# Queueing the taps of a depthwise convolution on VectorE behind given instructions of the MLP

## The chip, the cores and the metric

One core of a Trainium2 chip runs the whole network in one launch. The metric is the device time of that core in microseconds (us), the median over the runs shown; lower is better.

## What is computed

The input x is 1024 tokens by 1024 channels, float32, and goes through two layers and a last rmsnorm. Layer 0 is a hybrid mixer (a recurrence beside sliding-window attention) and an MLP; layer 1 is a convolution module and an MLP. The change touches what lies between the mixer's output and the second MLP. Cut to that:

```python
def conformer_conv(h, ...):
    u = h @ pw1_w + pw1_b
    u = u[..., :D_MODEL] * jax.nn.sigmoid(u[..., D_MODEL:])
    u = depthwise_conv(u, dw_w) + dw_b        # causal, 31 taps per channel
    u32 = layernorm(u, ln_g, ln_b)            # over the channels
    u = jax.nn.silu(u32)
    return u @ pw2_w + pw2_b

def sqrelu_mlp(h, w1, w2):                    # 1024 -> 4096 -> 1024
    return jnp.square(jax.nn.relu(h @ w1)) @ w2

x = x + mix;  x = x + sqrelu_mlp(rmsnorm(x), w1, w2)    # in each layer
```

## The kernel before, in words

Tokens are handled in two halves of 512, with channels on the 128 partitions: a half is eight tiles of 128x512 (`x0` for the first half, `x1` for the second). Every float32 product is made of three matmuls (`mm3`, lines 296 to 301): a number is split into a high part and the rest, and high by high, high by low and low by high are added up in PSUM. The high part is a cast on ScalarE (line 286 for weights), the low part a subtraction (`lo`, line 271), which goes to VectorE or to GpSimd by an argument; with `dve=False` it goes to GpSimd.

Weights come through SyncE's DMA queue into rings of four tiles for the raw values, the high and the low parts (`weights`, lines 273 to 291). One weight block of 8x128 channels uses two tiles of each ring, so at most two blocks are there at a time, and they come in the order of the program. Matmul results go to a ring of six PSUM banks (`self.mm`, line 1436).

The work around the change, in the order of the program (`run`, from line 1446):

- `conv_in(0)` (lines 1199 to 1217): the first projection of the convolution for the first half, eight channel tiles of 48 matmuls; each ends in one VectorE instruction that writes `u[c]` (line 1217).
- `mlp(0)` on `x1` (lines 1137 to 1196): eight blocks of 512 hidden channels. `first` makes a hidden piece (24 matmuls, then relu, square and the high part on ScalarE, the low part at line 1165 on GpSimd). `second` takes a block back to the channels in four groups of 24 matmuls; each group ends in two VectorE additions into `x` (line 1183), which also give two PSUM banks free. With `ahead` 2 the order is: four pieces; then for each block two pieces of the next, the four groups of this one, the other two pieces of the next.
- `conv(us, acc0)` (lines 1219 to 1227): 31 taps for each of eight channel tiles, 248 VectorE instructions, each `acc = u shifted * weight + acc` (line 1226; the first tap is line 1223).
- `conv_norm` (lines 1233 to 1252): layernorm and silu of the eight `acc` tiles, a chain over VectorE, TensorE (lines 1239 and 426) and ScalarE that ends in eight high and low parts (lines 1250 and 1251).
- `norm(x1)`, `conv_out(0)` (lines 1254 to 1263: eight columns of 24 matmuls, the last product of the convolution), copies of the last 30 columns of each `u[c]` to its front on GpSimd (line 1457).
- the same for the other half: `conv_in(1)`, `mlp(1)` on `x0` for seven of its blocks, `conv` of the second half, `conv_norm`, `conv_out(1)`, then the eighth block and the rest.

Up to the end of the mixer the order on TensorE is written out by hand. From there a planner orders every engine's queue when the kernel is built: it goes through its own estimate of the instructions' times, and gives an engine that is free the ready instruction that stands first in the program. The norms are marked as urgent. `conv` stands behind the whole MLP in the program, but its taps are ready as soon as `u[c]` is there, so the planner puts them on VectorE wherever it believes VectorE free. On the chip each engine then goes through its queue strictly in order.

Of the kernel before, what the change touches and what calls it, by code (L numbers as in the profile page):

```python
# [9 lines left out]
F32 = mybir.dt.float32  # L10
F32R = mybir.dt.float32r
AF = mybir.ActivationFunctionType
ALU = mybir.AluOpType
# [4 lines left out]
P = 128  # L18
D = 1024
S = 1024  # L20
H = 512
# [3 lines left out]
NTAP = 31  # L25
# [8 lines left out]
class Ring:  # L34
    """slots taken in turn, from one or several pools"""
# [10 lines left out]
class Net:  # L46
# [25 lines left out]
    # ---------------------------------------------------------------- order on the tensor engine  # L72
    def go(self, gen):
        """a stream on its own"""
        while True:
            try:
                next(gen)
            except StopIteration as e:
                return e.value

    def weave(self, base, *gens):
        """several streams in one order: the first of gens that is due goes on, base between them, so that the array
        stays busy; a stream yields the time (us) that its next products have to wait for the other engines, or the
        name of what has to be there"""
        due = [[0.0, g] for g in gens]
        rest = [[0.0, base]]
        share = 0.0

        def first(ds):
            return next((d for d in ds if (d[0] in self.done if isinstance(d[0], str) else d[0] <= self.clk)), None)  # L90

        while due or rest:
            f, b = first(due), first(rest)
            d = f if f and (share < LAG["SHARE"] or not b) else b
            if d is None:
                self.clk = min(d[0] for d in due + rest if not isinstance(d[0], str))
                continue
            t = self.clk
            try:
                w = next(d[1])  # L100
                d[0] = w if isinstance(w, str) else self.clk + w + (LAG["SLACK"] if w else 0.0)
            except StopIteration:
                (due if d is f else rest).remove(d)
            t = self.clk - t
            share = share + t if d is f else max(0.0, share - LAG["RATIO"] * t)

    # ---------------------------------------------------------------- constants
# [62 lines left out]
    def warm(self):  # L170
        """products that nobody reads, while the array would only wait: so its clock stays up for the first columns"""
        ps = self.mmps()
        for _ in range(4):
            self.nc.tensor.matmul(ps[:, 0:256], lhsT=self.ones, rhs=self.rst[:, 0:256], start=True, stop=True)
# [89 lines left out]
    # ---------------------------------------------------------------- helpers  # L264
    def lo(self, out, x, hi, dve=None):
        """out = x - hi, for the second part of an operand"""
        if dve is None:
            self.nlo += 1
            dve = self.nlo % 3 != 0
        eng = self.nc.vector if dve else self.nc.gpsimd  # L270
        eng.tensor_tensor(out=out, in0=x, in1=hi.bitcast(F32), op=ALU.subtract)  # L271

    def weights(self, aps, a, b, dve=None):
        """blocks of weights in two parts, k by k; loaded and split one half of them after the other"""
        nc = self.nc
        h = a // 2
        if dve is None:
            self.nlo += 1
            dve = self.nlo % 3 != 0
        ws = [([], []) for _ in aps]  # L280
        for i in range(2):
            for ap, (his, los) in zip(aps, ws):
                raw = self.wraw.tile([P, h, b], F32, "wraw")
                nc.sync.dma_start(out=raw, in_=ap[:, i * h:(i + 1) * h, :])
                hi = self.whi.tile([P, h, b], F32R, "whi")
                nc.scalar.copy(out=hi, in_=raw)  # L286
                lo = self.wlo.tile([P, h, b], F32R, "wlo")
                self.lo(lo, raw, hi, dve)
                his += [hi[:, k, :] for k in range(h)]
                los += [lo[:, k, :] for k in range(h)]  # L290
        return ws
# [30 lines left out]
    def norm_first(self, hf, rows, dst):  # L322
        """first rmsnorm by rows, then turned to feature-major; dst(u, g): where the two parts go"""
# [42 lines left out]
    def first_stored(self):  # L366
        """the second half's first norm, kept in DRAM until its place is free"""
# [20 lines left out]
    def colsum(self, xs, sq, k="n"):  # L388
        """sum over channels of x (or of its square), in two parts"""
# [29 lines left out]
    def rstd(self, accs, eps, pool, k="n"):  # L419
        """1 / sqrt(mean + eps) for every token, on every partition"""  # L420
# [56 lines left out]
    # ---------------------------------------------------------------- input projection  # L477
# [10 lines left out]
    def w_in_pair(self, js, hs):  # L488
        """two columns side by side, channel block by channel block: what is there first is used first"""
# [31 lines left out]
    # ---------------------------------------------------------------- rwkv  # L521
    def scan(self, hf, p, r, k, v, la, gl, sset, ptag, ahead):
# [86 lines left out]
        # unit lower triangular inverse: 16-blocks by substitution, then two merges  # L609
# [97 lines left out]
        # per chunk: state' = M state + C, output = R state + Y  # L707
# [114 lines left out]
    # ---------------------------------------------------------------- attention  # L822
    def attention(self, hf, i, z, qs, mi):
        """query heads 2i and 2i+1"""
# [54 lines left out]
    # ---------------------------------------------------------------- mixer of one half  # L879
# [14 lines left out]
    def shift(self, hf, j, ps, keep=False, hp=False):  # L894
        """one 128-channel column of the input projection of the rwkv part, shifted"""
# [18 lines left out]
    def twice(self, j, rows, cols, width):  # L914
        """64 channels of a column, on both halves of the partitions; cols: (from, of which half's column) pieces"""
# [6 lines left out]
    def att_in(self, hf):  # L922
        """keys with one block of the half before in front: the high part of each kv head on both halves of the
        partitions, the low parts of the first on the upper one and of the second on the lower one; values by rows"""
# [23 lines left out]
    def queries(self, hf, i, z):  # L948
        """two heads' queries, each with its high part on the half of the partitions where the low part of its keys is
        and its low part on the other one"""  # L950
# [10 lines left out]
    def att(self, hf, z):  # L961
        """attention of one half: query heads 4z to 4z+3"""
# [26 lines left out]
    def cols0(self, hs):  # L989
        """the first half's input projection"""  # L990
# [23 lines left out]
    def last1(self, h1):  # L1014
        """the last two columns, under the norm"""
# [20 lines left out]
    def scans(self, z, todo):  # L1036
        """scans one after the other in one set of tiles"""
# [39 lines left out]
    def w_out(self, hf, mi, xs, w_):  # L1077
        """output projection; the second half's input is there, the first half's comes along;
        the first half's first two columns begin with what is done, while the last scan and the attention go on"""
# [56 lines left out]
    # ---------------------------------------------------------------- mlp  # L1136
    def mlp(self, layer, halves, blocks, ahead, dve=None, close=None):
        """halves: list of (x tiles, (hi, lo)); blocks of 512 hidden channels;
        ahead: how many 128-channel pieces of a block go before the second product of the block in front;
        close: takes the second product of the last block"""  # L1140
# [5 lines left out]
        def first(fb, fts):  # L1146
            hid = hids.setdefault(fb, [([], []) for _ in halves])
            for ft in fts:
                f = fb * 4 + ft
                whi, wlo = self.weight(w1[:, :, f * P:(f + 1) * P], NK, P, dve)  # L1150
                for hh, (xs, (his, los)) in zip(hid, halves):
# [13 lines left out]
                    self.lo(lo, t, hi, dve)  # L1165
                    hh[0].append(hi)
                    hh[1].append(lo)

        def second(fb):
            hid = hids.pop(fb)  # L1170
            for oc in range(4):
                whi, wlo = self.weight(w2[:, fb * 4:fb * 4 + 4, oc * 256:(oc + 1) * 256], 4, 256, dve)
                for hh, (xs, _) in zip(hid, halves):
# [7 lines left out]
                    for o in range(2):  # L1181
                        x = xs[oc * 2 + o]
                        nc.vector.tensor_tensor(out=x, in0=pss[o], in1=x, op=ALU.add)  # L1183
# [14 lines left out]
    # ---------------------------------------------------------------- convolution  # L1198
    def conv_in(self, hf, hs, us):
# [3 lines left out]
        for c in range(NK):  # L1203
# [13 lines left out]
            nc.vector.scalar_tensor_tensor(out=u[:, NTAP - 1:], in0=ps, scalar=self.pv("b1", c), in1=t, op0=ALU.add, op1=ALU.mult)  # L1217

    def conv(self, us, accs):
        nc = self.nc  # L1220
        for c in range(NK):
            u, acc = us[c], accs[c]
            nc.vector.tensor_scalar(out=acc, in0=u[:, 0:H], scalar1=self.pv("dw0", c), scalar2=self.pv("db", c),
                                    op0=ALU.mult, op1=ALU.add)
            for j in range(1, NTAP):
                nc.vector.scalar_tensor_tensor(out=acc, in0=u[:, j:j + H], scalar=self.pv(f"dw{j}", c), in1=acc,  # L1226
                                               op0=ALU.mult, op1=ALU.add)

# [36 lines left out]
    def row_rstd(self, ss, n):  # L1265
        """1 / sqrt(mean + eps) from n sums of squares of every row"""
# [10 lines left out]
    def final(self, hf, xs):  # L1277
        """last rmsnorm, by rows again"""
# [19 lines left out]
    def final_rows(self, hf, xs, w2, his, los):  # L1298
        """what is there so far by rows, and the second product of the last block by rows; then the last rmsnorm, one
        block of tokens after the other"""  # L1300
# [50 lines left out]
    # ---------------------------------------------------------------- the whole  # L1351
    def run(self):
# [96 lines left out]
        self.conv_in(0, self.norm(x0, "nm1", 0), us)  # L1449
        self.go(self.mlp(0, [(x1, self.norm(x1, "nf0", 1))], range(8), 2, False))  # L1450
        acc0 = [self.mip.tile([P, H], F32, name="acc", tag="mi") for _ in range(8)]
        self.conv(us, acc0)
# [5 lines left out]
        self.conv_in(1, n1, us)  # L1458
        n0 = self.norm(x0, "nf1", 0)
        self.go(self.mlp(1, [(x0, n0)], range(7), 2, False))  # L1460
        acc1 = [self.mip.tile([P, H], F32, name="acc", tag="mi") for _ in range(8)]
        self.conv(us, acc1)
# [41 lines left out]
```

## Time and profile before

| | |
|---|---|
| runs | 2525.11, 2516.49 and 2522.08 us, median 2522.08 |
| profiled execution, from its first to its last instruction | 2519.2 us (the page gives no other time of that execution) |
| TensorE matmul busy | 2355.4 us, 93% |
| VectorE busy | 1568.6 us, 62% |
| ScalarE busy | 1055.3 us, 42% |
| GpSimd busy | 843.9 us, 33% |
| the 480 taps of line 1226 | 466.7 us of VectorE, 1030 ns each |

Busy time says how long an engine had an instruction in it, not that it worked at its full pace: matmuls overlap in their pipeline, so the pace of TensorE is read from the number of matmuls in a stretch, and an instruction that waits inside an engine for a port counts as busy. The mean granted TensorE clock is 0.968 of full speed.

### The profile page before, as it was taken

Reading aid. Unit: us, or ns where it says so; the run is one execution under the profiler, and the core shown is the slowest. Engines: PE = TensorE matmul, PEld = TensorE weight load, DVE = VectorE, ACT = ScalarE, POOL = GpSimd, SP = SyncE. Lnnn points to the kernel's source line nnn. Section 1 sums busy time; section 2 is a strip of 40 time slices with the busy share of each in tenths; the row PEclk is TensorE's granted clock in tenths of the full one; section 3 lists DMA queues with packets and bytes.
Section 4 is the critical chain, followed back from the end, with each engine's and each line's share of the span. In section 5 each row is a group of like instructions: output and inputs, shape, how many; then the busy total and the mean of one; then the engine's idle time right before and its main releaser. Section 6 shows DMA issues by size and latency. Waiting matters only on the chain.

```text
span 2519.2 us, 38162 instructions
## 1 busy us (share of the span) xinstructions
PE 2355.4 (93%) x14525; PEld 1875.1 (74%) x14525; DVE 1568.6 (62%) x2613; ACT 1055.3 (42%) x1888; POOL 843.9 (33%) x676
## 2 busy tenths in 40 slices
PE   7999899899999999999678999997779999999998
PEld 6776677767777778777566888876657888888887
DVE  6766745647573646499998403899998025533333
ACT  6546645445352424344223543523225434433333
POOL 2223333111111112126547664226456643212221
PEclk9999999989999999999898999999889999999999
DMA  6435324313122223323112333332222332433332
GB/s 210 115 108 147 93 67 147 101 58 90 56 70 85 74 81 101 101 84 101 59 59 76 101 98 99 93 88 84 67 67 80 101 100 88 127 100 96 97 99 85
DMA packets 371851, 236.19 MB, mean 94 GB/s; under 512 B 39522, under 2 KB 355156, under 8 KB 371668
## 3 DMA queue, kind: packets, MB, share of 16 engines
q1 hardware_dynamic: 367604, 225.89, 30.2%
q0 software_dynamic: 2176, 4.19, 0.6%
q10 hardware_dynamic: 1888, 3.67, 0.4%
q8 instruction: 114, 1.87, 0.3%
q14 instruction: 69, 0.57, 0.1%
HBM read 215.35 MB, written 18.35 MB: 93 GB/s over the span
## 4 chain that ended last, share of the span: by engine, by line
PE 64%; DVE 28%; ACT 3%; DMA 3%; issue 2%; SPq 0%; POOL 0%; ACTq 0%; DVEq 0%; POOLq 0%
PE mm L299 19%; PE mm L300 18%; PE mm L301 18%; DVE acc L1226 17%; DVE x L1183 1%; DVE wlo L271 1%; DVE nt L472 1%; PE sc L603 1%; DMA raw<-p 1%; PE sc L685 1%; DVE E L662 1%; DVE C L660 1%; DVE h L271 1%; PE sc L768 1%; PE at L842 1%
## 5 line engine op out<-in xcount | busy, mean ns | idle before, releaser
L271 POOL TENSOR_TENSOR wlo<-wraw,whi 128x512 fp32r<-128x512 f32 x448 | 630.6, 1411 | 1293.6 <-ACT whi L286 1223.3
L286 ACT CAST whi<-wraw 128x512 fp32r<-128x512 f32 x720 | 445.1, 620 | 1065.8 <-PE mm L300 911.0
L299 PE MATMUL mm<-h,whi 128*128 128x512 f32 x1792 | 730.3, 408 | 10.7 <-DVE x L1183 7.1
L301 PE MATMUL mm<-h,wlo 128*128 128x512 f32 x1792 | 707.2, 395 | 7.5 <-DVE wlo L271 7.5
L300 PE MATMUL mm<-h,whi 128*128 128x512 f32 x1792 | 706.4, 394 | 0.5 <-DVE h L271 0.3
L299 PE MATMUL mm<-hidh,whi 128*128 128x512 f32 x992 | 396.0, 401 | 77.0 <-DVE x L1183 75.4
L1226 DVE SCALAR_TENSOR_TENSOR acc<-u,par,acc 128x512 f32<-128x512 f32 x480 | 466.7, 1030 | 0.1
L299 PEld LDWEIGHTS mm<-h,whi 128*128 128x128 f32 x1792 | 340.5, 190 | 93.6 <-issue 18.1
L301 PEld LDWEIGHTS mm<-h,wlo 128*128 128x128 f32 x1792 | 340.4, 190 | 85.3 <-DVE wlo L271 11.6
L301 PE MATMUL mm<-hidh,wlo 128*128 128x512 f32 x992 | 389.8, 395 | 11.2 <-POOL wlo L271 11.2
L300 PEld LDWEIGHTS mm<-h,whi 128*128 128x128 f32 x1792 | 341.3, 190 | 67.8 <-issue 2.0
L300 PE MATMUL mm<-hidl,whi 128*128 128x512 f32 x992 | 390.0, 394 | 0.3 <-DVE hidl L271 0.2
L1183 DVE TENSOR_TENSOR x<-mm,x 128x512 f32<-128x512 f32 x248 | 167.6, 685 | 291.9 <-PE mm L301 291.7
L271 DVE TENSOR_TENSOR wlo<-wraw,whi 128x512 fp32r<-128x512 f32 x272 | 194.6, 717 | 202.7 <-ACT whi L286 194.4
L299 PEld LDWEIGHTS mm<-hidh,whi 128*128 128x128 f32 x992 | 189.3, 191 | 123.1 <-issue 80.7
L301 PEld LDWEIGHTS mm<-hidh,wlo 128*128 128x128 f32 x992 | 189.1, 191 | 52.2 <-POOL wlo L271 11.6
L300 PEld LDWEIGHTS mm<-hidl,whi 128*128 128x128 f32 x992 | 189.6, 191 | 39.8 <-issue 1.1
L271 POOL TENSOR_TENSOR hidl<-rel,hidh 128x512 fp32r<-128x512 f32 x77 | 113.1, 1468 | 44.3 <-ACT hidh L1162 25.1
L1158 ACT ACTIVATE rel<-rel 128x512 f32<-128x512 f32 x128 | 80.6, 632 | 3.5
L1157 ACT ACTIVATE rel<-mm 128x512 f32<-128x512 f32 x128 | 75.5, 592 | 5.9 <-DVE u L1217 4.8
L1164 DVE CAST hidh<-rel 128x512 fp32r<-128x512 f32 x68 | 31.4, 464 | 52.5 <-ACT rel L1158 52.4
L473 ACT CAST h<-nt 128x512 fp32r<-128x512 f32 x48 | 29.7, 621 | 56.9 <-DVE nt L472 56.5
(357 smaller groups left out, 2257.3 us busy)
## 6 DMA issues: line engine op xcount, KB each, us to landing
wraw<-in_mlp_w_dram SPq DMA_DIRECT2D x512, 256.0 KB
wraw<-in_cv_pw_w_dram SPq DMA_DIRECT2D x96, 256.0 KB
wraw<-in_hy_w_in_dram SPq DMA_DIRECT2D x80, 256.0 KB
wraw<-in_hy_w_out_dram SPq DMA_DIRECT2D x32, 256.0 KB
p<-stg SPq DMA_DIRECT2D x30, 256.0 KB
raw<-p SPq DMA_DIRECT2D x40, 128.0 KB
krv<-p SPq DMA_DIRECT2D x18, 256.0 KB
xrow<-in_x_dram SPq DMA_DIRECT2D x8, 512.0 KB
```

The lines of the kernel that those rows point to most:

```text
L271: eng.tensor_tensor(out=out, in0=x, in1=hi.bitcast(F32), op=ALU.subtract)
L286: nc.scalar.copy(out=hi, in_=raw)
L299: mm(ps, lhsT=whi, rhs=xhi, start=start, stop=False)
L300: mm(ps, lhsT=whi, rhs=xlo, start=False, stop=False)
L301: mm(ps, lhsT=wlo, rhs=xhi, start=False, stop=stop)
L472: nc.vector.scalar_tensor_tensor(out=t, in0=xs[c], scalar=self.pv(gname, c), in1=r, op0=ALU.mult, op1=ALU.mult)
L473: nc.scalar.copy(out=his[c], in_=t)
L1157: nc.scalar.activation(out=t, in_=ps, func=AF.Relu)
L1158: nc.scalar.activation(out=t, in_=t, func=AF.Square)
L1164: nc.vector.tensor_copy(out=hi, in_=t)
L1183: nc.vector.tensor_tensor(out=x, in0=pss[o], in1=x, op=ALU.add)
L1226: nc.vector.scalar_tensor_tensor(out=acc, in0=u[:, j:j + H], scalar=self.pv(f"dw{j}", c), in1=acc, op0=ALU.mult, op1=ALU.add)
```

## The change

The taps become a generator that stops after each tap. `beside(gen, rate)` gives a function that is called with an instruction; each call adds `rate` to an account, and for each whole one in it one more tap is traced, with an edge that keeps it behind that instruction in VectorE's queue (the order alone: it does not wait for the instruction's end). The calls are: after each `u[c]` of `conv_in` (5 taps a call in the first half, 6 in the second), after the low part of each hidden piece of the MLP, and after each pair of additions into `x` (3.6 taps a call in the first half, 4 in the second). What is left of the taps follows after the MLP. The account of `conv_in` and that of the MLP are separate. With `beside` given, the low part of a hidden piece goes to VectorE instead of GpSimd. The `acc` tiles are allocated ahead of `conv_in`. The rest of the diff takes out comments.

```diff
-    def mlp(self, layer, halves, blocks, ahead, dve=None, close=None):
+    def mlp(self, layer, halves, blocks, ahead, dve=None, close=None, beside=None):
...
-                    self.lo(lo, t, hi, dve)
+                    last = self.lo(lo, t, hi, True if beside else dve)
                     hh[0].append(hi)
                     hh[1].append(lo)
+                    if beside:
+                        beside(last)
...
-                        nc.vector.tensor_tensor(out=x, in0=pss[o], in1=x, op=ALU.add)
+                        last = nc.vector.tensor_tensor(out=x, in0=pss[o], in1=x, op=ALU.add)
+                    if beside:
+                        beside(last)
...
-            nc.vector.scalar_tensor_tensor(out=u[:, NTAP - 1:], in0=ps, scalar=self.pv("b1", c), in1=t, op0=ALU.add, op1=ALU.mult)
+            last = nc.vector.scalar_tensor_tensor(out=u[:, NTAP - 1:], in0=ps, scalar=self.pv("b1", c), in1=t, op0=ALU.add,
+                                                  op1=ALU.mult)
+            if beside:
+                beside(last)
+
+    def beside(self, gen, rate):
+        owed = [0.0]
+
+        def run(behind):
+            owed[0] += rate
+            with self.tc.issue_after(behind.ins):
+                while owed[0] >= 1.0:
+                    owed[0] -= 1.0
+                    next(gen, None)
+
+        return run
...
             nc.vector.tensor_scalar(out=acc, in0=u[:, 0:H], scalar1=self.pv("dw0", c), scalar2=self.pv("db", c),
                                     op0=ALU.mult, op1=ALU.add)
+            yield
             for j in range(1, NTAP):
                 nc.vector.scalar_tensor_tensor(out=acc, in0=u[:, j:j + H], scalar=self.pv(f"dw{j}", c), in1=acc,
                                                op0=ALU.mult, op1=ALU.add)
+                yield
...
-        self.conv_in(0, self.norm(x0, "nm1", 0), us)
-        self.go(self.mlp(0, [(x1, self.norm(x1, "nf0", 1))], range(8), 2, False))
         acc0 = [self.mip.tile([P, H], F32, name="acc", tag="mi") for _ in range(8)]
-        self.conv(us, acc0)
+        conv = self.conv(us, acc0)
+        self.conv_in(0, self.norm(x0, "nm1", 0), us, self.beside(conv, 5))
+        self.go(self.mlp(0, [(x1, self.norm(x1, "nf0", 1))], range(8), 2, False, beside=self.beside(conv, 3.6)))
+        self.go(conv)
...
-        self.conv_in(1, n1, us)
+        acc1 = [self.mip.tile([P, H], F32, name="acc", tag="mi") for _ in range(8)]
+        conv = self.conv(us, acc1)
+        self.conv_in(1, n1, us, self.beside(conv, 6))
         n0 = self.norm(x0, "nf1", 0)
-        self.go(self.mlp(1, [(x0, n0)], range(7), 2, False))
-        acc1 = [self.mip.tile([P, H], F32, name="acc", tag="mi") for _ in range(8)]
-        self.conv(us, acc1)
+        self.go(self.mlp(1, [(x0, n0)], range(7), 2, False, beside=self.beside(conv, 4)))
+        self.go(conv)
```

## Rows read from the trace of the kernel before

**Rows 1.** The page's part 2: busy tenths in 40 slices of 63 us.

```profile
PE   7999899899999999999678999997779999999998
...
DVE  6766745647573646499998403899998025533333
```

**Rows 2.** Stretches: start:end, length, each engine's busy us and instruction count, granted clock, DMA.

```profile
1060.00:1170.00 110.00, 104.72 (x454) 84.71 (x454) 106.83 (x128) 46.44 (x76) 37.03 (x26) 1.00 0.31 88
1170.00:1370.00 200.00, 151.73 (x613) 122.01 (x612) 197.10 (x214) 57.22 (x95) 119.60 (x74) 0.87 0.22 68
1370.00:1563.00 193.00, 193.00 (x851) 159.51 (x850) 59.12 (x71) 90.86 (x152) 114.56 (x87) 1.00 0.31 96
1563.00:1607.00 44.00, 44.00 (x194) 36.08 (x193) 31.62 (x40) 20.90 (x36) 13.34 (x9) 1.00 0.34 98
1607.00:1718.00 111.00, 108.52 (x472) 87.75 (x471) 105.15 (x126) 41.55 (x66) 38.08 (x24) 1.00 0.32 92
1718.00:1905.00 187.00, 134.60 (x558) 109.29 (x557) 186.31 (x202) 51.10 (x85) 92.56 (x59) 0.86 0.22 69
1905.00:2066.00 161.00, 161.00 (x706) 132.84 (x706) 52.09 (x60) 75.76 (x127) 99.08 (x74) 1.00 0.31 96
```

**Rows 3.** TensorE's waits from 1060 to 2070 us: total, times, longest.

```profile
PE mm L299 <- DVE x L1183: 82.6, 7, 23.4
PE mm L301 <- POOL wlo L271: 11.2, 1, 11.2
PE mm L301 <- DVE wlo L271: 7.5, 9, 1.9
PE lnl L1239 <- DVE acc L1238: 6.9, 2, 3.9
```

**Rows 4.** Timeline of VectorE, then of TensorE, around the first long wait.

```profile
1194.37 23.93 DVE L1226 SCALAR_TENSOR_TENSOR acc<-u,par,acc 128x512 f32<-128x512 f32 x36
1218.22 0.67 DVE L1183 TENSOR_TENSOR x<-mm,x 128x512 f32<-128x512 f32 x1
...
1200.39 0.39 PE L301 MATMUL mm<-hidh,wlo 128*128 128x512 f32 x1
1219.04 0.77 PE L299 MATMUL mm<-hidh,whi 128*128 128x512 f32 x1 [18.27 <-DVE x L1183]
```

**Rows 5.** The stretch just after that wait, as in rows 2.

```profile
1219.50:1223.50 4.00, 4.00 (x11) 3.00 (x11) 4.00 (x5) 0.00 (x0) 4.00 (x4) 0.50 0.44 129
```

**Rows 6.** Timelines of VectorE and GpSimd: taps alone, taps against GpSimd, a waiting copy.

```profile
1317.33 10.02 DVE L1226 SCALAR_TENSOR_TENSOR acc<-u,par,acc 128x512 f32<-128x512 f32 x15
...
1303.49 10.28 DVE L1226 SCALAR_TENSOR_TENSOR acc<-u,par,acc 128x512 f32<-128x512 f32 x6
...
1302.93 1.79 POOL L271 TENSOR_TENSOR hidl<-rel,hidh 128x512 fp32r<-128x512 f32 x1
...
1309.79 3.44 POOL L271 TENSOR_TENSOR wlo<-wraw,whi 128x512 fp32r<-128x512 f32 x2
...
1321.45 6.57 POOL L1457 COPY u<-u 128x30 f32<-128x30 f32 x1 [6.51 <-DVE acc L1226]
```

**Rows 7.** Groups of GpSimd, 1370 to 1560 us (few taps): count, busy, mean ns.

```profile
L271 POOL TENSOR_TENSOR wlo<-wraw,whi 128x512 fp32r<-128x512 f32 x68 | 90.1, 1328 | 57.7 <-ACT whi L286 56.9 <-PE mm L301 0.7
```

**Rows 8.** Groups of VectorE, 1607 to 1718 us, as in rows 7.

```profile
L1226 DVE SCALAR_TENSOR_TENSOR acc<-u,par,acc 128x512 f32<-128x512 f32 x75 | 72.2, 1007 | 0.0
L271 DVE TENSOR_TENSOR wlo<-wraw,whi 128x512 fp32r<-128x512 f32 x19 | 12.9, 680 | 2.3 <-ACT whi L286 2.3
```

**Rows 9.** VectorE's timeline: last taps and last low parts of both convolution norms.

```profile
1357.37 1.55 DVE L1226 SCALAR_TENSOR_TENSOR acc<-u,par,acc 128x512 f32<-128x512 f32 x2
...
1406.38 4.08 DVE L271 TENSOR_TENSOR h<-acc,h 128x512 fp32r<-128x512 f32 x3
...
1898.14 0.73 DVE L1226 SCALAR_TENSOR_TENSOR acc<-u,par,acc 128x512 f32<-128x512 f32 x1
...
1947.37 1.18 DVE L271 TENSOR_TENSOR h<-acc,h 128x512 fp32r<-128x512 f32 x1
```

More of the change, by code (lines that the diff above doesn't have):

```diff
@@ L270, in lo @@
         eng = self.nc.vector if dve else self.nc.gpsimd
-        eng.tensor_tensor(out=out, in0=x, in1=hi.bitcast(F32), op=ALU.subtract)
+        return eng.tensor_tensor(out=out, in0=x, in1=hi.bitcast(F32), op=ALU.subtract)
     def weights(self, aps, a, b, dve=None):
@@ L1196, in mlp, with conv_in @@
                 yield from first(blocks[i + 1], range(ahead, 4))
-    def conv_in(self, hf, hs, us):
+    def conv_in(self, hf, hs, us, beside=None):
         nc = self.nc
```

## Prediction

> **What bounds the kernel now.** I began with the page's slices [rows 1]: TensorE stands at 8 or 9 tenths nearly everywhere, and drops to 6 or 7 in two places, in slices 20 to 22 and 28 to 30. There VectorE stands at 8 or 9, and the granted clock drops to 0.87 and 0.86 [rows 2]. Those are the two convolutions. So TensorE bounds the kernel, and in these two places VectorE holds it up.
>
> How much is lost is read from the stretches [rows 2]. Undisturbed, TensorE starts 851 matmuls in 193 us, one every 0.2268 us. From the first matmul of conv_in(0) to the last of mlp(0) (1060 to 1563 us) there are 454 + 613 + 851 = 1918, worth 435 us; they take 503. From conv_in(1) to the end of the seven blocks (1607 to 2066) there are 472 + 558 + 706 = 1736, worth 394; they take 459. Lost: 68 + 65 = **133 us**. Of this about 11 lie in the two conv_in stretches (110 against 454 matmuls' 103, 111 against 472 matmuls' 107); the rest lies where the MLP runs beside the taps. conv_out(0), 44 us, loses nothing.
>
> What TensorE waits for [rows 3]: 82.6 us for the additions into x (line 1183) in only seven waits, 11.2 in one wait for a low part of weights from GpSimd, 7.5 for those from VectorE, 6.9 for the norm. The first long wait shows why [rows 4]: TensorE stops at 1200.8 us, and the addition that would give its bank free stands in VectorE's queue behind 36 taps that run for 23.9 us. Six banks allow about five groups of 12 matmuls, 5 x 2.72 = 13.6 us, of delay; 24 is more. The taps filled gaps that the planner saw and the chip does not have. After the wait the clock is granted at 0.50, the lower of TensorE's two levels, for some 4 us [rows 5]: 11 matmuls at twice their time, 2 us more. The 82.6 us are the waits alone; such stretches make up part of the rest.
>
> Why the chip lags the planner [rows 6]: 15 taps run in 10.02 us, 0.67 each, while GpSimd only waits. Six taps against six GpSimd subtractions take 10.28 us, 1.71 each. So while one of these two works on two SBUF inputs the other waits, and a GpSimd subtraction costs VectorE 1.71 - 0.67 = 1.04 us.
>
> **The change, step by step.**
>
> *Where the taps go.* A hidden piece is 24 matmuls, 5.44 us, and so is a group of the second product. In the first half conv_in takes 8 x 5 = 40 taps, and the MLP's 64 calls could take 3.6 each; 208 are left, so call 58 takes the last. In the second half 48 go in conv_in, and of 56 calls with 4 each the 50th takes the last. At most 4 taps (6 in conv_in) now stand ahead of an addition or a low part: 4 x 1.71 = 6.8 us at worst, inside the 13.6 us that the banks allow. So the long waits of [rows 3] go. The taps issue no DMA, and no queue but VectorE's is passed; the acc tiles are free (w_out has read what was in them before conv_in(0) begins; in the second half the first taps need conv_norm(0), which stands before conv_in(1) anyway).
>
> *Is VectorE fast enough?* A call has 5.44 us. VectorE has 3.6 x 0.67 = 2.4 us of taps (second half 4 x 0.67 = 2.7), and on average of a low part (0.68, [rows 8]) and two additions (2 x 0.67, [rows 4]) 1.0; sum 3.4 or 3.7, about 65% of the time. Each call also has two weight tiles whose low parts GpSimd makes. Each costs VectorE at most 1.04, and about 0.65 x 1.04 = 0.68 if it meets VectorE only when that has work. Sum: 4.8 to 5.5 us in the first half (88 to 101%), 5.1 to 5.8 in the second (93 to 106%). Too slow by at most 0.06 x 58 + 0.34 x 50 = 20 us, at best by nothing. Nearest is the middle of both, where VectorE keeps up and only its queue is uneven: I take 8. The move of 32 + 28 low parts from GpSimd to VectorE is in this sum; it takes 1.04 of GpSimd's use of the inputs away for 0.68 of VectorE's.
>
> *conv_in.* 48 taps stand in the second one in place of 75 [rows 8], 40 in the first; I leave 6 of the 11 us (bounds 3 and 11).
>
> *The copies of line 1457* wait in GpSimd's queue for a channel's last tap, 6.5 us in [rows 6], ahead of low parts of weights; that is where the 11.2 us of [rows 3] come from. With VectorE a few us behind the planner, some of it stays: 4 (between 0 and 11).
>
> *What is late next: conv_norm.* Before, it ended some 150 and 120 us ahead of the MLP's end and cost almost nothing. From the last tap to its last low part it takes 1410.5 - 1358.9 = 51.5 us and 1948.6 - 1898.9 = 49.7 [rows 9]. Now the last call has two pieces and four groups of MLP behind it, 6 x 5.44 = 32.6 us, and the norm's own matmuls (about 2): TensorE is done 34.6 us after the call. The additions and last taps take 4, so the last low part is there at about 55.5 (second half 53.7). The first column of conv_out needs all eight parts, so it ends at 56 (54) instead of 34.6 + 5.4 = 40: 16 and 14 us lost, and 2 each at the lower clock [rows 5]: 34. Nothing fills this gap: with two weight blocks at a time, in the order of the program, conv_out's weights hold the rings, and neither conv_in(1) nor the eighth block can start. If the first two columns go through their products in turn, it is 5.4 less at each, 23; if the norm runs faster beside fewer other instructions, near 10. The norm of x1, late before, now runs under this gap and conv_out's 44 us.
>
> *Sum.* Left of the 133 us: 6 + 8 + 4 + 34 = 52. Gain 81. 2519.2 - 81 = 2438. The median of the runs shown is 2.9 above this span: **2441 us**.
>
> **A rule against it.** In the row GpSimd's subtraction costs VectorE 1.04 us, less than the 1.33 it lasts when few taps run [rows 7]; a part of it overlaps with the tap. The Trainium skill, "SBUF — State Buffer", section "Who interferes with whom", says that a VectorE instruction with two SBUF inputs and a GpSimd one that reads SBUF exclude each other for the whole instruction. The row agrees that they exclude each other, not that it is for the whole length. What the whole length would give is the second rival.
>
> **The rivals.**
> 1. *The gap is closed better.* The norm's chain shortens or the columns interleave, and VectorE keeps up: 3 + 3 + 0 + 10 = 16 left, gain 117, 2405 us. For it: at 1370 to 1563 TensorE loses nothing with GpSimd 59% busy [rows 2]. Against: 50 us of chain in both instances. Chance 0.14.
> 2. *The two engines exclude each other for GpSimd's whole 1.33 us.* Then a call costs VectorE 3.4 + 2.7 = 6.1 us, or 6.4: 0.66 x 58 + 0.96 x 50 = 86 us in place of 8. Left 130, gain 3: 2519 us. For it: VectorE is at 5.1 to 5.8 of 5.44 anyway. Against: six pairs in 10.28 us [rows 6]. Chance 0.06.
> 3. *Slower: conv_norm lies open.* If the last taps come after the MLP's end, its whole chain is idle time for TensorE, twice. Its price is a delay of the last tap: 52 left become 133 when both come 40 us later than I reckon, 44 us after the call, which is 10 us after TensorE's end. That takes 40 / 58 = 0.7 us a call more on VectorE, a GpSimd subtraction priced near 1.3 to 1.4 us instead of 0.7 to 1.04. At 60 us later each, left are 172: 2561 us. For it: VectorE near 100%, and its lag adds up over 50 calls. Against: [rows 6], and VectorE stood only part of each call against GpSimd. Chance 0.08.
> 4. *The change does not do what it says*: the order is set by the planner's times, and the additions still come late, behind other work. 2522 us. Against: the edges and the account limit a burst to 6 taps whatever the planner believes. Chance 0.04.
>
> **The numbers.** The forecast has 0.68, and by the bounds above it runs from 2412 (3 + 0 + 0 + 20 left of the 133) to 2478 (11 + 20 + 11 + 46 left, the last if both last taps come 6 us later). A measurement of this kernel tells about 0.3%, 7.5 us, from no change. Faster: the forecast and rival 1, and a little of rival 2: 0.84. Same: rival 4 and most of rival 2: 0.08. Slower: 0.08. The range runs from rival 1 to a little past the forecast's upper bound, 2403 to 2490, and leaves out rivals 2 to 4, 0.18.
>
> **What would show it.** Right: the groups of 20 and more taps ahead of line 1183 are gone, the longest wait for it is a few us; TensorE keeps about 4.4 matmuls per us in both MLP stretches; VectorE's mean tap stays near 1 us, and VectorE is at 9 tenths over whole stretches of 435 and 390 us instead of 290; TensorE stands idle, once after each MLP, for some 15 us, waiting for the norm's chain or its low parts. Wrong: TensorE spread thin over the MLP with many waits for line 1183 (VectorE too slow, rival 2); gaps of 50 us before conv_out (rival 3); no gap there at all (rival 1).

## The result and the profile after

Measured: 2415.5 us median (2409.26 to 2416.73) against 2519.28 us for the kernel before, a ratio of 0.9584 with a 95% interval of 0.9561 to 0.9606, so 104 us or 4.2% faster. The forecast was 2441 us, with a range from 2403 to 2490. In a later comparison on one chip with other kernels the change gave 0.9585 (0.956 to 0.9611).

The page's part 2 of the changed kernel answers to [rows 1]; a slice is now 60 us.

```profile
PE   7999999989999999999999998999999989999998
...
DVE  6766844657656464558888888889999976433333
```

The two hollows of TensorE are gone but for an 8 in slice 25 and one in slice 33. VectorE no longer goes 9, 9, 9, 9 and then 4; it stands at 8 or 9 all the way through both MLPs.

The stretches of the changed kernel, with columns as in [rows 2]: conv_in(0) with the MLP, conv_out(0), conv_in(1), the MLP's seven blocks, conv_out(1).

```profile
1068.00:1501.00 433.00, 431.36 (x1898) 355.75 (x1896) 368.94 (x420) 182.46 (x299) 205.49 (x149) 1.00 0.32 96
1501.00:1557.00 56.00, 50.55 (x211) 40.78 (x211) 49.99 (x62) 33.39 (x58) 17.73 (x12) 0.94 0.27 80
1557.00:1650.00 93.00, 93.00 (x410) 76.66 (x409) 77.85 (x93) 36.70 (x58) 26.13 (x18) 1.00 0.33 97
1650.00:1953.00 303.00, 298.46 (x1311) 245.40 (x1309) 293.97 (x307) 122.85 (x203) 162.78 (x108) 1.00 0.32 98
1953.00:2007.00 54.00, 48.87 (x200) 39.61 (x201) 29.91 (x40) 23.93 (x40) 12.42 (x9) 0.91 0.27 78
```

At 0.2268 us a matmul, 2.5 us are lost in the first of them (433 against 1898 x 0.2268), 8.1 at conv_out(0), nothing in conv_in(1), 5.7 in the second MLP stretch (most of it at its end, where the norm's matmuls come) and 8.6 at conv_out(1). That is 25 us in place of 133. TensorE's clock is granted in full in both MLP stretches, where it was 0.87 and 0.86 on average beside the taps.

TensorE's waits of the changed kernel from 1060 to 2000 us, the answer to [rows 3].

```profile
PE mm L299 <- ACT h L1273: 13.1, 2, 6.7
PE lnl L1262 <- DVE acc L1261: 1.7, 1, 1.7
PE mm L300 <- POOL h L271: 1.5, 3, 0.6
```

Not one wait for an addition into x is left, nor one for a low part of weights. What is left is above all two waits of 6 to 7 us for the first high part of the convolution's norm (line 1273, line 1250 before): conv_out now waits for the norm, once in each half, as forecast, but not for as long.

The timeline of VectorE in the changed kernel around that first gap: the last taps of the first half, the last low part of the norm, the ends of the first two columns of conv_out; then the last taps and the last low parts of the second half.

```profile
1466.40 2.52 DVE L1248 SCALAR_TENSOR_TENSOR acc<-u,par,acc 128x512 f32<-128x512 f32 x3
...
1515.94 1.78 DVE L271 TENSOR_TENSOR h<-acc,h 128x512 fp32r<-128x512 f32 x1
...
1520.23 0.74 DVE L1286 SCALAR_TENSOR_TENSOR x<-mm,par,x 128x512 f32<-128x512 f32 x1
...
1522.45 0.74 DVE L1286 SCALAR_TENSOR_TENSOR x<-mm,par,x 128x512 f32<-128x512 f32 x1
...
1920.55 3.10 DVE L1248 SCALAR_TENSOR_TENSOR acc<-u,par,acc 128x512 f32<-128x512 f32 x4
...
1961.10 5.27 DVE L271 TENSOR_TENSOR h<-acc,h 128x512 fp32r<-128x512 f32 x5
```

The first norm takes 1517.7 - 1468.9 = 48.8 us, the second 1966.4 - 1923.7 = 42.7; [rows 9] gave 51.5 and 49.7. The first two columns end 2.2 us apart and not 5.4: their products were done in turn, as each part of the norm came.

### The profile page after: what moved, and what is told of

It is laid out like the page before. It is cut to its first block, busy times and chain, and to the rows that moved or that the text cites. A ratio compares the mean times of both kernels' runs of the same rounds, so it can differ in the third digit from the quotient of the medians.

```text
span 2414.3 us, 38159 instructions
## 1 busy us (share of the span) xinstructions
PE 2337.3 (97%) x14525; PEld 1865.0 (77%) x14525; DVE 1636.3 (68%) x2673; ACT 1056.8 (44%) x1888; POOL 746.6 (31%) x616
## 4 chain that ended last, share of the span: by engine, by line
PE 72%; DVE 19%; DMA 3%; ACT 3%; issue 2%; POOL 1%; SPq 0%; ACTq 0%; POOLq 0%; DVEq 0%
PE mm L299 21%; PE mm L300 20%; PE mm L301 20%; DVE acc L1248 9%; DVE x L1186 1%; DVE hidl L271 1%; DMA raw<-p 1%; PE sc L603 1%; PE sc L685 1%; DVE E L662 1%; PE sc L768 1%; PE at L842 1%; DVE C L660 1%; PE at L874 1%; PE sc L722 1%
## 5 line engine op out<-in xcount | busy, mean ns | idle before, releaser
L1248 DVE SCALAR_TENSOR_TENSOR acc<-u,par,acc 128x512 f32<-128x512 f32 x480 | 505.1, 1053 | 10.7
L299 PE MATMUL mm<-hidh,whi 128*128 128x512 f32 x992 | 390.0, 395 | 2.3 <-DVE hidh L1165 1.7
L271 DVE TENSOR_TENSOR hidl<-rel,hidh 128x512 fp32r<-128x512 f32 x111 | 87.1, 785 | 37.1 <-ACT hidh L1163 35.7
L769 DVE TENSOR_TENSOR st<-sc,C 128x64 f32<-128x64 f32 x64 | 14.1, 221 | 61.5 <-PE sc L768 61.2
```

The source lines that it names most:

```text
L271: return eng.tensor_tensor(out=out, in0=x, in1=hi.bitcast(F32), op=ALU.subtract)
L299: mm(ps, lhsT=whi, rhs=xhi, start=start, stop=False)
```

## The experiments

Two theories of why the kernel before lost time were open after this. In the **order theory** (the prediction's own) the long rows of taps ahead of an addition do it. In the **load theory** the spread of the load and the low parts that left GpSimd do it. The first four runs made a third necessary, the **wrong-times theory**, which stands behind them.

**Taps let out in bursts.** The account is the change's, but in the MLP stretches taps are let out only when 36 (or 14) are owed.

```diff
     def run(behind):
         owed[0] += rate
+        if owed[0] < min(burst, left[0]):
+            return
```

> The changed kernel with the same taps per call in the account, but in the MLP stretches they are let out 36 at a time, behind every tenth (ninth) call, so the same work stands on VectorE in the same stretches in long runs. Order theory (TensorE is lost when more taps stand ahead of an addition into x than the six PSUM banks allow, 13.6 us): a run of 36 lasts 24 to 38 us, TensorE stands still 10 to 24 us at each of some ten runs, 100 to 200 us in all: 2515 to 2615 us, near the kernel before or slower. Load theory (the gain comes from spreading the load and moving low parts off GpSimd, whatever the length of a run): within 15 us of the changed kernel, 2415 to 2430 us.

> As the runs of 36, but 14 taps at a time. Order theory: a run lasts 9.4 us alone and 14 to 16 us where GpSimd takes part, about what the banks allow (13.6 us): 0 to 40 us slower than the changed kernel, 2415 to 2455 us, and clearly below the runs of 36. Load theory: 2415 us, the same as the runs of 36.

Bursts of 36: 2480.7 us, ratio 0.9856 (0.9835 to 0.9877). Bursts of 14: 2440.2 us, 0.9695 (0.968 to 0.971). The medians are ordered as the order theory has them, and 14 lies in its range; 36 lies between the ranges of both theories, and the place is wrong. Stretches of the run with bursts of 36: inside the first MLP, around conv_out(0), inside the second MLP, around conv_out(1).

```profile
1170.00:1480.00 310.00, 302.53 (x1319) 249.33 (x1318) 259.75 (x276) 115.24 (x191) 164.73 (x116) 0.99 0.31 94
1480.00:1560.00 80.00, 54.91 (x217) 41.51 (x217) 68.73 (x83) 36.84 (x60) 18.73 (x13) 0.83 0.19 56
1660.00:1960.00 300.00, 292.56 (x1270) 240.95 (x1268) 249.49 (x257) 113.74 (x188) 153.26 (x106) 0.98 0.31 93
1960.00:2060.00 100.00, 69.94 (x277) 54.74 (x276) 72.56 (x95) 37.52 (x60) 22.63 (x17) 0.83 0.21 64
```

Inside the MLPs 310 - 1319 x 0.2268 = 11 and 300 - 1270 x 0.2268 = 12 us were lost, not the 100 to 200 expected. Around the two conv_outs it was 31 and 37, where the change loses 8 and 9: in the first half 28 taps were still owed at call 58 and ran until 1502.7 us instead of 1468.9. So this run gives the price of a late last tap, some 23 us for 34 us later, and says less than I meant it to about long rows: on VectorE no more than eight taps stand in a row ahead of an addition into x, and no more than twelve ahead of a low part of a hidden piece. Taps that are let out together are not a block. Each waits for the one before it, and the planner puts what is ready in between.

**The low parts of the hidden pieces, alone.** First the change without their move to VectorE (a copy of one column takes their place as the instruction to queue behind), then the kernel before with the move and nothing else.

```diff
-                    last = self.lo(lo, t, hi, True if beside else dve)
+                    self.lo(lo, t, hi, dve)
...
+                        beside(nc.vector.tensor_copy(out=mark, in_=hi.bitcast(F32)[:, 0:1]))
```

```diff
-                    self.lo(lo, t, hi, dve)
+                    self.lo(lo, t, hi, True if dve is False else dve)
```

> The changed kernel with the low parts of the hidden pieces of these two MLP stretches back on GpSimd; the taps stand behind a copy of one column of the high part on VectorE instead, so the calls stay. Order theory: the move is worth little: 0 to 10 us slower than the changed kernel (a GpSimd subtraction costs VectorE up to 1.04 us against 0.68 for doing it itself), 2415 to 2425 us. Load theory: a good part of the 104 us comes from the move, 2440 to 2480 us.

> The kernel before with that move alone: low parts of the hidden pieces of the two MLP stretches on VectorE, the taps as early as they can run. Order theory: the long runs of taps ahead of the additions stay, 2500 to 2530 us. Load theory: 2440 to 2480 us.

Without the move: 2427.4 us (2418.2 to 2435.8), 0.9644 (0.9614 to 0.9673), 12 us more than the change, a little past the order theory's bound. With the move alone: 2499.6 us, 0.992 (0.9892 to 0.9948). Neither has the load theory's size. The second comes out at the lower end of the order theory's range, but by its trace not for that theory's reason: no more than six taps stand in a row ahead of an addition into x, and no more than twelve ahead of a hidden piece's low part. The kernel before has rows of 54, 53 and 35 ahead of an addition; the 36 of [rows 4] are what a view from 1195 us on shows of the first. The main parts of the first two (a first tap and seven taps stand ahead of each):

```profile
1180.46 37.83 DVE L1226 SCALAR_TENSOR_TENSOR acc<-u,par,acc 128x512 f32<-128x512 f32 x46
...
1728.25 42.31 DVE L1226 SCALAR_TENSOR_TENSOR acc<-u,par,acc 128x512 f32<-128x512 f32 x45
```

Yet the run with the move loses nearly as much, in many short waits. Its largest waits from 1060 to 2070 us, its stretch beside the taps, and the subtractions of GpSimd there:

```profile
PE mm L299 <- DVE x L1183: 30.4, 7, 6.8
PE mm L300 <- DVE hidl L271: 22.4, 7, 6.8
```

```profile
1170.00:1370.00 200.00, 166.74 (x667) 132.64 (x667) 199.60 (x227) 61.66 (x103) 99.19 (x64) 0.90 0.25 74
```

```profile
L271 POOL TENSOR_TENSOR wlo<-wraw,whi 128x512 fp32r<-128x512 f32 x56 | 92.4, 1661 | 52.6 <-ACT whi L286 52.6
```

Lost: 200 - 667 x 0.2268 = 49 us, with 56 subtractions on GpSimd and VectorE busy all the time. The rows alone don't do it: in the run with bursts of 36 they are as long, up to twelve, and where VectorE was busy 260 of 310 us and 249 of 300, TensorE lost 11 and 12. At the 1.04 us that a subtraction costs VectorE the 56 are 58 us. That price rests on six subtractions beside six taps; [rows 6] has three of the six, and these are the others:

```profile
1304.68 3.44 POOL L271 TENSOR_TENSOR wlo<-wraw,whi 128x512 fp32r<-128x512 f32 x2
1308.08 1.75 POOL L271 TENSOR_TENSOR hidl<-rel,hidh 128x512 fp32r<-128x512 f32 x1
```

In the kernel before, its two stretches [rows 2] hold 66 and 59 such subtractions by the groups of GpSimd below (the next run's expectation says 60 and 56), 69 and 61 us, and TensorE lost 61 and 60.

```profile
L271 POOL TENSOR_TENSOR wlo<-wraw,whi 128x512 fp32r<-128x512 f32 x52 | 84.5, 1637 | 20.2 <-ACT whi L286 20.0
L271 POOL TENSOR_TENSOR hidl<-rel,hidh 128x512 fp32r<-128x512 f32 x14 | 23.8, 1701 | 4.7 <-ACT hidh L1162 4.7
...
L271 POOL TENSOR_TENSOR wlo<-wraw,whi 128x512 fp32r<-128x512 f32 x47 | 74.4, 1589 | 88.6 <-ACT whi L286 88.1
L271 POOL TENSOR_TENSOR hidl<-rel,hidh 128x512 fp32r<-128x512 f32 x12 | 19.8, 1653 | 6.6 <-ACT hidh L1162 6.5
```

Hence the **wrong-times theory**: the planner fills VectorE to the last gap with times that leave out what GpSimd's subtractions cost. On the chip VectorE then falls behind by that cost, it has no gap in which to catch up, and TensorE, whose additions and low parts stand at their planned places in the queue, pays nearly all of it.

**No subtraction on GpSimd.** The kernel before, taps as early as they can run, with all low parts of the two MLP stretches on VectorE.

```diff
+        low = True if dve is False else dve
...
-                whi, wlo = self.weight(w1[:, :, f * P:(f + 1) * P], NK, P, dve)
+                whi, wlo = self.weight(w1[:, :, f * P:(f + 1) * P], NK, P, low)
...
-                whi, wlo = self.weight(w2[:, fb * 4:fb * 4 + 4, oc * 256:(oc + 1) * 256], 4, 256, dve)
+                whi, wlo = self.weight(w2[:, fb * 4:fb * 4 + 4, oc * 256:(oc + 1) * 256], 4, 256, low)
...
-                    self.lo(lo, t, hi, dve)
+                    self.lo(lo, t, hi, low)
```

> The kernel before, taps as early as they can run, but with every low part of the two MLP stretches (weights and hidden pieces) on VectorE, so that GpSimd has no subtraction beside the taps. Wrong-times theory (the planner orders VectorE's full queue with times that leave out what GpSimd's subtractions cost, 60 and 56 of them at 1.04 us in the two stretches, and TensorE loses just that, 56 and 58 us): without them the plan holds, TensorE loses next to nothing although VectorE stays full: 2395 to 2430 us. Full-engine theory (VectorE at 100% is itself what holds TensorE up; 116 subtractions of 0.68 us more on it make it worse): 2510 to 2560 us.

2408.9 us, 0.9574 (0.9554 to 0.9594): as fast as the change, with no tap held back. Stretches of this run beside the taps, then three of VectorE's groups in the first of them:

```profile
1170.00:1360.00 190.00, 188.93 (x826) 154.06 (x825) 187.16 (x294) 73.74 (x124) 33.01 (x8) 1.00 0.33 99
...
1700.00:1841.00 141.00, 140.53 (x615) 114.71 (x615) 137.43 (x217) 53.85 (x90) 0.00 (x0) 1.00 0.33 101
```

```profile
L1227 DVE SCALAR_TENSOR_TENSOR acc<-u,par,acc 128x512 f32<-128x512 f32 x164 | 115.7, 734 | 0.0
L271 DVE TENSOR_TENSOR wlo<-wraw,whi 128x512 fp32r<-128x512 f32 x71 | 47.9, 675 | 1.4 <-ACT whi L286 1.3
...
L271 DVE TENSOR_TENSOR hidl<-rel,hidh 128x512 fp32r<-128x512 f32 x20 | 13.5, 676 | 1.4 <-ACT hidh L1163 1.4
```

VectorE is busy 187 of 190 us, as full as before. It has 91 subtractions more, 71 for weights and 20 for hidden pieces, and still does 164 taps here, where the kernel before did 176 in the same 190 us. TensorE loses 190 - 826 x 0.2268 = 3 us. A full VectorE was not what held TensorE up; a tap took 734 ns on average and not 1041. The Trainium skill, "Perfetto Trace Analysis", section "Optimizing Scalar/DVE Operations", says that moving work between these two engines might not help, since they share an SBUF read port. Here moving the work back from GpSimd did help, by 107 us (2515.9, the median of before in that comparison, less 2408.9).

**More taps a call.** The change with 5 taps a call in both MLPs.

```diff
-        self.go(self.mlp(0, [(x1, self.norm(x1, "nf0", 1))], range(8), 2, False, beside=self.beside(conv, 3.6)))
+        self.go(self.mlp(0, [(x1, self.norm(x1, "nf0", 1))], range(8), 2, False, beside=self.beside(conv, 5)))
...
-        self.go(self.mlp(1, [(x0, n0)], range(7), 2, False, beside=self.beside(conv, 4)))
+        self.go(self.mlp(1, [(x0, n0)], range(7), 2, False, beside=self.beside(conv, 5)))
```

> The changed kernel with 5 taps a call in both MLP stretches in place of 3.6 and 4, never more than 6 in a row. Wrong-times theory: the plan still fits (5 x 0.67 + 1.02 = 4.4 of 5.44 us a call), but on the chip two subtractions of 1.04 us make it 6.45, so TensorE loses up to 1.0 us a call over 42 and 40 calls, 40 to 82 us, and gets back up to 23 us of the gaps ahead of conv_out, since the last taps come earlier: 2435 to 2480 us. Queue theory (only a long row of taps ahead of an addition costs anything): 2395 to 2415 us.

2460.9 us, 0.9782 (0.9759 to 0.9805): 45 us slower than the change by the medians, with rows no longer than seven ahead of an addition or a hidden piece's low part. TensorE's waits of this run, 1060 to 2070 us:

```profile
PE mm L299 <- DVE x L1186: 19.7, 7, 5.0
PE mm L301 <- POOL wlo L271: 12.7, 4, 3.9
PE lnl L1262 <- DVE acc L1261: 8.5, 2, 5.0
PE mm L300 <- DVE hidl L271: 8.1, 4, 2.6
```

The waits for line 1186 are back, each short, and no gap ahead of conv_out is left. The time is in the wrong-times theory's range and far from the queue theory's. So the rate of the change matters: at 3.6 and 4 the subtractions of GpSimd fit into the time that a call leaves, at 5 they don't.

**All low parts on VectorE, with the calls.** The change with the move of the run before last.

> The changed kernel, taps behind their calls, with every low part of the two MLP stretches on VectorE. Wrong-times theory: with nothing on GpSimd the calls have nothing left to mend; a call costs VectorE 3.6 x 0.67 + 1.02 + 2 x 0.68 = 4.8 us (second half 5.1) of 5.44, the plan holds, and the gaps ahead of both conv_out stay since the last taps stay where they are: 2405 to 2420 us, not better than the kernel before with the same move (2409). If keeping the taps back is worth something by itself: 2390 to 2402 us.

2411.7 us, 0.9573 (0.9546 to 0.96): the same as that move without calls. TensorE waits 14.7 us in two waits for the norm's high parts, as in the change, and for nothing else over 1.3 us. Where the planner's times hold, keeping the taps back gives nothing; it moves the loss to the gaps ahead of conv_out.

**The gaps ahead of conv_out.** The hidden pieces of the eighth block are moved ahead of conv_out(1), its second product stays behind; and the same with 4.1 taps a call in the first half.

```diff
-        self.go(self.mlp(1, [(x0, n0)], range(7), 2, False, beside=self.beside(conv, 4)))
+        self.go(self.mlp(1, [(x0, n0)], range(8), 2, False, close=keep, beside=self.beside(conv, 4)))
...
-        self.go(self.mlp(1, [(x0, n0)], [7], 0))
+        w2, his, los = kept[0]
+        for oc in range(4):
...
```

> The changed kernel with the four hidden pieces of the eighth block of mlp(1) on x0 moved ahead of conv_out(1), the block's second product staying behind it: 21.8 us of work for TensorE while the convolution's second norm runs. If the 14 us lost there are TensorE waiting for the norm: 6 to 14 us faster than the changed kernel, 2401 to 2410 us; 0 to 6 us may come back under the norm of x1, which is left with half of its cover. If the norm is not what it waits for: 2415 us.

> The pieces moved as in the run beside this, and 4.1 in place of 3.6 taps a call in the first half, so that its last tap stands behind call 51 and not 58, 38 us earlier. If the 9 us lost ahead of conv_out(0) are the wait for the norm, and VectorE at 4.1 still keeps up as it does at 4 in the second half: 4 to 9 us faster than the moved pieces alone, 2393 to 2405 us. If VectorE falls behind at 4.1: no faster, or slower.

Pieces moved: 2397.5 us (2391.3 to 2404.0), 0.9529 (0.9505 to 0.9553). Both: 2397.5 us, 0.9531 (0.951 to 0.9551). The move gives back 18 us by the medians, 14 by the ratios, against the 6 to 14 expected, and leaves a single wait of 6.5 us for line 1273, so the second gap was TensorE waiting for the norm. The 4.1 closes the first gap as well (no wait for line 1273), but gives nothing of the 4 to 9 us expected: there are waits for line 1186, for weights' low parts and for the norm's first sum in its place. 3.6 was already near what the first half allows.

**Calls in conv_in alone.** What was left in the run with no subtraction on GpSimd beside the MLP's taps stands at conv_in, where GpSimd still takes a third of the weights: 110 - 449 x 0.2268 = 8 us were lost from 1060 to 1170 us, and 105 - 435 x 0.2268 = 6 from 1555 to 1660, a little less than the 9 each of the expectation. Its waits are for the low parts that VectorE makes (1060 to 2070 us):

```profile
PE mm L301 <- DVE wlo L271: 12.2, 14, 1.8
```

There the calls are kept; beside the MLP the taps run as early as they can, with `low` used for all low parts of the two MLP stretches as above.

```diff
+        low = True if dve is False else dve
...
         self.conv_in(0, self.norm(x0, "nm1", 0), us, self.beside(conv, 5))
-        self.go(self.mlp(0, [(x1, self.norm(x1, "nf0", 1))], range(8), 2, False, beside=self.beside(conv, 3.6)))
+        self.go(self.mlp(0, [(x1, self.norm(x1, "nf0", 1))], range(8), 2, False))
...
-        self.go(self.mlp(1, [(x0, n0)], range(7), 2, False, beside=self.beside(conv, 4)))
+        self.go(self.mlp(1, [(x0, n0)], range(7), 2, False))
```

> The kernel before with every low part of the MLP stretches on VectorE, and calls in conv_in alone (5 and 6 taps a call): the other taps run as early as they can beside the MLP. Wrong-times theory: in the run without calls TensorE lost 9 us in each conv_in, where GpSimd still takes a third of the weights' low parts beside the taps, and next to nothing after it; held back there, some 12 of these 18 us come back, and no gap appears ahead of conv_out: 2392 to 2402 us. If the conv_in loss has another cause (VectorE's own low parts behind the norm): 2405 to 2412 us.

> The changed kernel itself, beside the two others on one chip: 2410 to 2420 us by every theory.

2391.2 us (2384.1 to 2398.5), 0.9499 (0.9475 to 0.9523), beside 2414.5 us and 0.9585 (0.956 to 0.9611) for the change in the same comparison: 23 us faster than the change, 128 faster than before, a little better than expected. Stretches of this run: conv_in(0), beside the taps, conv_in(1), beside the taps.

```profile
1064.00:1170.00 106.00, 106.00 (x468) 87.40 (x467) 97.47 (x138) 49.09 (x80) 16.89 (x12) 1.00 0.32 93
1170.00:1370.00 200.00, 199.48 (x871) 162.54 (x870) 198.12 (x312) 75.24 (x126) 20.93 (x7) 1.00 0.33 99
1550.00:1660.00 110.00, 110.00 (x487) 91.07 (x486) 105.87 (x146) 43.31 (x72) 18.05 (x12) 1.00 0.32 91
1660.00:1840.00 180.00, 179.52 (x783) 146.00 (x782) 178.02 (x280) 68.85 (x116) 0.00 (x0) 1.00 0.33 98
```

VectorE is full beside the MLP, TensorE loses 2.5 us at most in each stretch, and no gap stands ahead of conv_out. This is near all that there was: 2519 - 133 is 2386. That GpSimd's third is what cost TensorE time in conv_in is argued; the calls also take taps from ahead of VectorE's own low parts, and moving that third alone was not tried.

## Why the prediction was right, and where it was off

**The loss before.** 133 us were found from the count of matmuls, and 25 are left in the change: 108 back, against 105 between the two spans. The place and the size of what could be won were right.

**Its cause.** The prediction had the step "the taps filled gaps that the planner saw and the chip does not have", and the price of a subtraction on GpSimd, 1.04 us. The price is borne out: by it 58, 69 and 61 us in the three stretches that were counted, of which TensorE lost 49, 61 and 60. What failed is the step that made the length of a row decide ("six banks allow 13.6 us; 24 is more"). The row of 36 taps of [rows 4] is there, in truth 54 long, but it is how the delay came out in one place. With rows of six at most ahead of an addition and VectorE full, the run with the low parts of the hidden pieces moved lost 49 us in the stretch where the kernel before lost 61, and the run with 5 taps a call lost 45 against the change. What decides is whether VectorE keeps up with its queue when each subtraction beside it costs 1.04 us; with taps behind calls that means staying under 5.44 us a call. That was the second question of the prediction, "is VectorE fast enough", and it was the main one. That the planner leaves these costs out is argued from the runs with no subtraction, in which its order holds with VectorE full; its times themselves were not read.

**The terms.** 6 + 8 + 4 + 34 = 52 us were forecast as left; measured are 25. *VectorE too slow*, 8: in the first half nothing can be seen (2.5 us for conv_in and MLP together); in the second 5.7, much of it the norm's own wait. VectorE was busy 294 of 303 us in the second MLP, inside the 93 to 106% that the rows gave, and that cost TensorE little. *conv_in*, 6: nothing in the second half, next to nothing in the first. *The copies*, 4: GpSimd waited 14.4 us for taps ahead of them, but TensorE never waited for GpSimd's low parts of weights. *The gap ahead of conv_out*, 34: about 17 at the two conv_outs and a few at the MLP's end before the second. This is the term that was most mis-sized. The columns did go in turn, the case priced at 23; I had taken the other one because weights stand in the order of the program, but two blocks of weights are there at a time, and the planner uses both. The norms were also 2.7 and 7 us shorter than in [rows 9].

**The rivals.** The first, 2405 us with a well closed gap, was nearest in kind: most of the terms went its way. The second, in which the two engines exclude each other for GpSimd's whole 1.33 us, did not happen at 3.6 and 4 taps a call: it asked for over 6 us a call, and the MLP ran at full pace. The Trainium skill, "SBUF — State Buffer", section "SBUF: two separate sides", has the exclusion for the whole instruction; the trace has the exclusion, and 1.04 us of it. The third, slower, has its mechanism shown in the run with bursts of 36, where a last tap 34 us later cost 23 us in one half; in the change the last tap came at 1468.9 us, 30 us ahead of the MLP's last matmul.

## What to carry to other kernels

When a planner orders the queues, look for costs that it can't see, and above all for two engines that exclude each other: an engine that the plan fills completely has no gap to catch up in, so nearly all of such a cost goes to the engine that the kernel is bound by. Leaving gaps (here by letting the taps out at a given rate) mends it, but taking away the hidden cost mends it better: with the subtractions on VectorE the plan held at 99% busy, and only conv_in, where some of the hidden cost remained, was still worth holding back. Price the gaps by the count of matmuls in a stretch, and before blaming the longest row in a queue, shorten the row alone.

## What the runs showed of the hardware

A copy of 128x30 elements on GpSimd, 0.2 us at its shortest, takes many times as long while VectorE runs taps without a break: 6.57 us in [rows 6]. In the run with all low parts on VectorE it is longer still; line 1458 there (minimum, median, longest in ns):

```profile
L1458 POOL COPY u<-u x8: 210/975/14650, 1206.7 to 1355.3; 128x30 f32<-128x30 f32 x8
```

So a short instruction of GpSimd can stand for 14.65 us beside a VectorE that goes from one instruction with two SBUF inputs to the next, where a subtraction of 128x512 got its turn after each tap [rows 6]. This is the longest copy, and the VectorE instruction that was running when it ended:

```profile
1268.56 14.65 POOL L1458 COPY u<-u 128x30 f32<-128x30 f32 x1 [61.20 <-DVE acc L1227]
...
1283.06 0.67 DVE L1184 TENSOR_TENSOR x<-mm,x 128x512 f32<-128x512 f32 x1
```

Each of the three copies over 2 us in this run (14.65, 12.72 and 2.60) ended about 0.15 us after an addition into x began, the first VectorE instruction in that time with an input in PSUM. The copy of [rows 6] ended without one. Why the copy and the subtraction differ was not tried. Nothing waited for these copies here.
